# Conditioning units, the scan's steps and the first MLP pairs of a hybrid flow backbone

## The chip, the core and the metric

One core of one Trainium2 chip runs the whole program: a denoising step of a two-layer backbone on 512 latent and 128 context tokens. The metric is the device time of one execution in microseconds (us), the median of several. The engines are TensorE (PE; its weight loads are PEld), VectorE (DVE), ScalarE (ACT), GpSimd (POOL), and SyncE (SP), whose queue issues nearly all DMA transfers in program order.

## What is computed

Each layer computes six conditioning vectors per channel from `c` (and `c_ctx` for the context), a modulated norm, one wide input projection, three token mixers, an output projection, and an MLP with squared ReLU. The kernel gives the same outputs for the tokens, the keys and values and the final scan states:

```
mod = silu(c) @ w_mod[l] + b_mod[l]            # sh1, sc1, g1, sh2, sc2, g2 = split(mod, 6)
h = rmsnorm(x, ln1) * (1 + sc1) + sh1
a_qkv, a_z, a_beta, a_alpha, b_q, b_k, b_v, c_q, c_k, c_v, gates = split(h @ w_in)
ya = gated delta rule, both directions (8 heads of 64, chunks of 64 tokens)
yb, yc = global and windowed attention
x = x + g1 * ((sig(ga)*(ya@w_br_a) + sig(gb)*(yb@w_br_b) + sig(gc)*(yc@w_br_c)) @ w_o)
h2 = rmsnorm(x, ln2) * (1 + sc2) + sh2
x = x + g2 * (square(relu(h2 @ w_ff1)) @ w_ff2)

def step(s, xs):                               # the scan over chunks, s_0 from the context's scan
    u = up_c - w_c @ s
    o = q_c @ s + a_c @ u
    s_new = gl * s + k_c^T @ u                 # = (gl - k_c^T w_c) s + k_c^T up_c
    return s_new, o
```

The conditioning is 12 units per layer of 512 channels each: sh1 and sc1 are units 0 to 3, g1 units 4 and 5, sh2 and sc2 units 6 to 9, g2 units 10 and 11.

## The kernel before

Activations lie feature-major: channels on the 128 partitions, 640 tokens along a row, worked on in two halves of 320. Large products run on pairs of fp32r numbers, a high and a low part, as three products (hi x hi, hi x lo, lo x hi), summed in one PSUM bank. A weight block of fp32 comes by DMA (`fraw`, `graw`, `wraw`), ACT casts it to the high part (L167) and POOL or DVE subtracts that for the low part (L168). Products of the projections appear in the trace as L189 (`gemm_fm`), those of the fills as L422; a product of plain fp32 leaves two PE instructions for each matmul.

**Order.** The program is written in generators that are woven together, and a scheduler then orders each engine's instructions by their priorities and by its own timeline; work with a low priority (`OFF`) goes where the rest leaves room. The low-priority work of a layer is 36 *fills* (`unit`, L415): the parts of the input projection that are needed late. Each takes two weight blocks from a ring of three buffers (`FR`), and SP's nops pace them (L201). DMA issues stand on SP in the order in which the program sets them.

**Conditioning units.** `mod_unit` (L247) sums one unit: eight loads of `w_mod` of 256 KB into the same `fraw` ring, for each four fp32 matmuls of 32 weight columns (L255), then a copy on ACT, a transpose on PE and small adds on DVE (`mod_finish`). In layer 0 units 0 to 3 run at the very start with larger loads. The other eight are low-priority work: unit 4 ahead of all fills (`MP = 1`), and units 5 to 11 one after every fourth fill (`MS = 4`). Layer 1's units run on DVE during layer 0's MLP (`mod_sum`).

**Delta rule.** Four pairs of heads per layer. For each there are the features (convolution and norms), a preparation, a triangular solve, five *posts* (one per 128 tokens, two chunks each), the scan, and the output. The posts of one pair run beside the features and the preparation of the next. `gdn_post` (L608) ends with one bank per chunk that holds the transition matrix of both directions and the additive term; DVE adds the decay to the first (`wm`, L689) and ACT copies the second (`bb`, L690), each as one instruction for both directions, since direction 0 lies on partitions 0 to 63 and direction 1 on 64 to 127. The scan (L698) takes nine steps, seven with a latent chunk of each direction and two for the context. Forward chunk `cf` and backward chunk `cb_` differ, so a step is four products of 64x64 (L712: two heads, two directions) and two adds on DVE of 64 partitions (L716). The states of all chunks stay in `H`; a block of products with `qe` reads them out at the end.

**Output projection and MLP.** `ws` loads the output projection's eight weight blocks through a ring of six buffers and three raw ones; the eight products of the first token half follow, then those of the second, with the next norm between them. The MLP works by pairs of 128-wide hidden blocks. `ff1_plain(p)` takes the two weights of pair p one after the other, each for both halves.

## Time and profile before

| | us |
|---|---|
| median of three runs (lowest, highest) | 2790.38 (2784.02, 2794.83) |
| the profiled execution | 2789.14 |
| its span in the trace | 2787.4 |
| PE busy | 2640.4 (95%) |
| DVE busy | 1986.0 (71%) |
| ACT busy | 1206.7 (43%) |
| POOL busy | 953.4 (34%) |

The stages, as times from the span's start: the start up to the first product of the delta rule; delta rule of layer 0 from 51.7 to 585.7, attention to 890.7, output projection from 922.5 to 982, MLP from 988; in layer 1 the delta rule from 1438.4 to 1978, attention to 2253.8, then projections and MLP up to the end. The fills run within delta rule and attention.

In a row of the timeline, the first number is the start, the second the length of a stretch of like instructions (xN of them), then engine, line, operation, output and inputs by the program's names; in brackets the engine's idle time before it and what ended that. A table of stretches gives for each engine the busy time and the instructions, and PEclk, the granted clock of TensorE as a share of full speed.

### The profile page before, as it was taken

The page shows a single profiled execution, that of the slowest core. Times are in us where ns is not written, and L with a number is a line of the kernel's source. Part 1 is how long each engine was busy: PE and PEld are TensorE (multiplying, and loading weights), DVE is VectorE, ACT ScalarE, POOL GpSimd, SP SyncE. Part 2 cuts the span into 40 slices and gives each one's busy share as a digit, 9 for nine tenths or more (in the row PEclk, how much of TensorE's full clock was granted, in tenths as well). Part 3 has the DMA queues.
Part 4 walks back from the last instruction along what each step waited for, and adds up shares of the span by engine and source line. Part 5 has one row for each costly group of instructions (what it writes and reads, how often), then busy time and mean ns, then how long its engine had stood idle before and what let it go on. Part 6 is the DMA issues. An engine that isn't in the chain of part 4 may idle for free. (4 is left out here: it accounts for less than half of the span.)

```text
span 2787.4 us, 55620 instructions
## 1 busy us (share of the span) xinstructions
PE 2640.4 (95%) x21108; PEld 2450.0 (88%) x21108; DVE 1986.0 (71%) x4253; ACT 1206.7 (43%) x2846; POOL 953.4 (34%) x1259
## 2 busy tenths in 40 slices
PE   5989999999999999999999899899999999999999
PEld 4887888888978999999989888888998789999999
DVE  4587897655557678999966888976556776676564
ACT  3434434445544343444344345344455454343342
POOL 1434434454444211122124445344644630111110
PEclk9999999999999999999999999999999999999999
DMA  7222212333234323554522211112323242222231
GB/s 249 86 89 63 90 47 67 116 118 93 79 103 153 127 79 108 150 159 148 152 85 77 80 48 58 51 48 95 102 72 110 69 154 71 66 85 75 69 99 61
DMA packets 117145, 268.62 MB, mean 96 GB/s; under 512 B 13712, under 2 KB 22544, under 8 KB 116880
## 3 DMA queue, kind: packets, MB, share of 16 engines
q1 hardware_dynamic: 116880, 265.08, 29.8%
q8 instruction: 167, 2.74, 0.4%
q14 instruction: 98, 0.80, 0.1%
HBM read 232.52 MB, written 32.51 MB: 95 GB/s over the span
## 5 line engine op out<-in xcount | busy, mean ns | idle before, releaser
L422 PE MATMUL fm<-hh,fhi 128*128 128x320 f32 x2304 | 446.2, 326 | 17.2 <-SPq L201 8.1
L422 PEld LDWEIGHTS fm<-hh,fhi 128*128 128x128 f32 x2304 | 363.9, 196 | 32.1 <-issue 8.6
L168 POOL TENSOR_TENSOR rl<-fr,rh 128x320 fp32r<-128x320 f32 x128 | 141.5, 1111 | 677.1 <-ACT rh L167 677.0
L168 POOL TENSOR_TENSOR flo<-fraw,fhi 128x512 fp32r<-128x512 f32 x176 | 237.4, 1350 | 306.8 <-ACT fhi L167 189.4
L167 ACT CAST ghi<-graw 128x1024 fp32r<-128x1024 f32 (+1 forms) x148 | 144.9, 980 | 226.1 <-PE gm L1249 128.3
L422 PE MATMUL fm<-hh,flo 128*128 128x320 f32 x1152 | 235.3, 326 | 4.0 <-SPq L201 2.9
L1098 DVE SCALAR_TENSOR_TENSOR x<-gm,mod,x 128x320 f32<-128x320 f32 (+2 forms) x384 | 153.7, 431 | 85.2 <-PE gm L1249 84.5
L1249 PE MATMUL gm<-rh,ghi 128*128 128x320 f32 x1024 | 195.5, 310 | 3.1 <-DVE x L1098 2.9
L1249 PE MATMUL gm<-rl,ghi 128*128 128x320 f32 x1024 | 196.6, 310 | 0.0
L168 DVE TENSOR_TENSOR glo<-graw,ghi 128x1024 fp32r<-128x1024 f32 (+1 forms) x148 | 170.5, 1153 | 35.4 <-ACT ghi L167 18.7
L422 PEld LDWEIGHTS fm<-hh,flo 128*128 128x128 f32 x1152 | 183.8, 195 | 11.0 <-SPq L201 4.8
L1249 PE MATMUL gm<-rh,glo 128*128 128x320 f32 x1024 | 192.0, 309 | 0.0
L167 ACT CAST fhi<-fraw 128x512 fp32r<-128x512 f32 x192 | 119.0, 620 | 162.1 <-PE fm L422 84.9
L189 PE MATMUL mb<-hh,whi 128*128 128x320 f32 x1024 | 167.8, 313 | 3.2 <-ACT whi L167 3.2
L1249 PEld LDWEIGHTS gm<-rh,ghi 128*128 128x128 f32 x1024 | 160.9, 188 | 5.4 <-DVE x L1098 2.4
L1249 PEld LDWEIGHTS gm<-rl,ghi 128*128 128x128 f32 x1024 | 161.7, 188 | 1.0 <-issue 1.0
L1249 PEld LDWEIGHTS gm<-rh,glo 128*128 128x128 f32 x1024 | 160.8, 188 | 0.0
L189 PEld LDWEIGHTS mb<-hh,whi 128*128 128x128 f32 x1024 | 152.5, 188 | 7.2 <-ACT whi L167 4.0
L270 DVE SCALAR_TENSOR_TENSOR macc<-fraw,csil,macc 128x512 f32<-128x512 f32 x168 | 134.9, 820 | 0.2 <-DMA fraw<-w_mod 0.2
L1187 PE MATMUL gm<-hh,ghi 128*128 128x320 f32 x768 | 130.2, 310 | 0.0
L598 DVE TENSOR_TENSOR sv<-sv,stmp 128x31 f32<-128x31 f32 (+15 forms) x248 | 123.4, 498 | 6.5
L961 DVE TENSOR_REDUCE mx<-s 128x1 f32<-128x640 f32 (+3 forms) x160 | 100.1, 632 | 36.6 <-PE s L951 22.6
(326 smaller groups left out, 6210.8 us busy)
## 6 DMA issues: line engine op xcount, KB each, us to landing
graw<-w_ff SPq DMA_DIRECT2D x128, 512.0 KB, 3.5
fraw<-w_mod SPq DMA_DIRECT2D x160, 256.0 KB, 2.8
fraw<-w_fm SPq DMA_DIRECT2D x144, 256.0 KB, 2.8
f_spill<-fgt SPq DMA_DIRECT2D x72, 320.0 KB, 2.2
wraw<-w_fm SPq DMA_DIRECT2D x32, 512.0 KB, 3.5
gts<-f_spill SPq DMA_DIRECT2D x48, 320.0 KB, 3.1
fraw<-w_br SPq DMA_DIRECT2D x48, 256.0 KB, 2.7
graw<-w_o SPq DMA_DIRECT2D x20, 512.0 KB, 4.8
```

The costliest lines, as they stand in the source:

```text
L167: ACT.copy(hi, src)
L168: (lo_eng or DVE).tensor_tensor(out=lo, in0=src, in1=hi.bitcast(F32), op=SUB)
L189: mm = PE.matmul(ps, lhsT=w_[k], rhs=x_[:, k, s], start=(i == 0 and k == 0), stop=(i == 2 and k == n - 1))
L270: stt(out=a, in0=raw, scalar=c, in1=a, op0=MUL, op1=ADD)
L422: mm = PE.matmul(ps[half], lhsT=w[:, k], rhs=x_[:, 4 * q + k, s], start=(q == 0 and k == 0 and w is hi and x_ is hh), stop=(q == 1 and k = ...
L598: tt(out=XX[:, s + 1:32, 0:m], in0=XX[:, s + 1:32, 0:m], in1=tv, op=SUB)
L961: DVE.tensor_reduce(out=mx, in_=pv, axis=AX.XY if n > 512 else AX.X, op=ALU.max)
L1098: stt(out=x[:, j, a:b], in0=ps[:, a - t0:b - t0], scalar=gate[:, j, c:c + 1], in1=x[:, j, a:b], op0=MUL, op1=ADD)
L1187: PE.matmul(ps, lhsT=w_[:, 4 * q + k], rhs=x_[o][:, k], start=(first and i == 0 and k == 0), stop=(i == 2 and k == 3), skip_group_check=True)
L1249: PE.matmul(ps, lhsT=w_[k], rhs=r[k // 2][o][:, k % 2, half_of(half)], start=(i == 0 and k == 0), stop=(i == 2 and k == 3))
```

## The change

Three edits. *Units*: unit 4 no longer runs ahead of the fills (`MP = 0`), units 4 to 7 stand after every eighth fill (`MS = 8`), and units 8 to 11 after the products j = 0, 2, 4 and 6 of the first half of layer 0's output projection. *MLP*: `ff1_plain` takes pairs 0 and 1 together: all four weights for the first token half, then for the second. *Scan*: the transition matrices of step n go into one zeroed tile `wmd`, direction 0 and 1 as the diagonal blocks of a 128x128 matrix in the order of the steps, so that a step is two full-size products, one per head; the states of a step lie in `Hs`, and one add on 128 partitions makes the next. Two copies on ACT (`put`) spread each state into `H` by chunk for the read-out. Posts write each direction into its own place (`STEP_F`, `STEP_B`), so that a chunk takes two adds and two copies where it took one and one; the context's add and copy likewise. The ten buffers of `wm` and `bb` become one `wmd` and one `bbs`.

```diff
@@ -85,7 +85,7 @@
 MB, FM, FB, FR, OFF = 3, 2, 2, 3, 30000
 PACE, PG = 4, 2
 HK = (2, 4, 5)
-MS, MP = 4, 1
+MS, MP = 8, 0
 WRING = 6
 
 
@@ -346,7 +346,7 @@
             for u in range(4):
                 mod_unit(0, u, npool, 2, 6)
             istk.close()
-        mods = [(mod_unit, l, u) for u in range(4, 12)] if l == 0 else []
+        mods = [(mod_unit, l, u) for u in range(4, 8)] if l == 0 else []
         with tc.high_priority(offset=-OFF):
             for f, *a in mods[:MP]:
                 f(*a)
@@ -366,7 +366,7 @@
...
-        GB = dict(zz=2, dd=2, wraw=2, tm=NLB, at=NLB, gss=2, grs=2, sv=3, Y=2, kgb=2, qeg=2, r2=2, gi=2, gsq=2, kq=2, rm=2, rlb=2, ee=2, wm=5, bb=5, qe=5, op=2)
+        GB = dict(zz=2, dd=2, wraw=2, tm=NLB, at=NLB, gss=2, grs=2, sv=3, Y=2, kgb=2, qeg=2, r2=2, gi=2, gsq=2, kq=2, rm=2, rlb=2, ee=2, qe=5, op=2)
...
@@ -657,8 +657,6 @@
                 return Y[:, u, 64:128]
 
             yield
-            wm = gtile([P, 2, 2, 64], "wm")
-            bb = gtile([P, 2, 2, 64], "bb")
             gi = gtile([P, 2, 2, 64], "gi")
             tt(out=gi, in0=bc(egs[:, :, t, h2], 3, 64), in1=bc(bc(i64, 1, 2), 1, 2), op=MUL)
             pqo = bank([P, 3, P], "ma")
@@ -686,41 +684,47 @@
                     PE.matmul(po[64 * h:64 * h + 64], lhsT=yv(u), rhs=AB[:, u], start=(dd == 0), stop=(dd == 1))
             yield
             for c in range(2):
-                tt(out=wm[:, c], in0=pwb[c][:, 0], in1=gi[:, c], op=ADD)
-                ACT.copy(bb[:, c], pwb[c][:, 1])
+                for dd, st in ((0, STEP_F), (1, STEP_B)):
+                    n, o = st[2 * t + c], slice(64 * dd, 64 * dd + 64)
+                    if n is not None:
+                        tt(out=wmd[o, n, :, o], in0=pwb[c][o, 0], in1=gi[o, c], op=ADD)
+                        ACT.copy(bbs[o, n], pwb[c][o, 1])
             yield
             qe = gtile([P, 2, P], "qe")
             ACT.copy(qe, pq)
             ACT.copy(opt[:, t], po)
             busy[pr["ix"]] = dbusy[i] = False
-            res[t] = dict(wm=wm, bb=bb, qe=qe)
+            res[t] = dict(qe=qe)
 
         def gdn_scan(hp, post, opt, oh):
-            H = gtile([P, 10, 2, 64], "H")
+
+            H, Hs = (gtile([P, 10, 2, 64], n) for n in ("H", "Hs"))
             Hf = gtile([P, 2, 64], "Hf")
             h2 = slice(2 * hp, 2 * hp + 2)
-            nc.sync.dma_start(out=H[0:64, 0], in_=d["state"][l, 0:64, h2])
-            nc.sync.dma_start(out=H[64:128, 7], in_=d["state"][l, 64:128, h2])
+            nc.sync.dma_start(out=Hs[:, 0], in_=d["state"][l, :, h2])
+            POOL.memset(Hs[:, 8], 0.0)
             POOL.memset(H[0:64, 8], 0.0)
             POOL.memset(H[64:128, 9], 0.0)
 
-            def step(cf, cb_, of, ob):
+            def put(n, cf, cb_):
+                ACT.copy(H[0:64, cf], Hs[0:64, n])
+                ACT.copy(H[64:128, cb_], Hs[64:128, n])
+
+            def step(n, i, o):
                 ps = bank([P, 2, 64], "ma")
                 for h in range(2):
-                    for dd, c in ((0, cf), (1, cb_)):
-                        s = slice(64 * dd, 64 * dd + 64)
-                        PE.matmul(ps[s, h], lhsT=post[c // 2]["wm"][s, c % 2, h], rhs=H[s, c, h],
-                                  start=True, stop=True)
-                for dd, c, o in ((0, cf, of), (1, cb_, ob)):
-                    s = slice(64 * dd, 64 * dd + 64)
-                    tt(out=o[s], in0=ps[s], in1=post[c // 2]["bb"][s, c % 2], op=ADD)
-
+                    PE.matmul(ps[:, h], lhsT=wmd[:, n, h], rhs=Hs[:, i, h], start=True, stop=True)
+                tt(out=o, in0=ps, in1=bbs[:, n], op=ADD)
+
+            put(0, 0, 7)
             for n in range(7):
-                step(n, 7 - n, H[:, n + 1], H[:, 6 - n])
+                step(n, n, Hs[:, n + 1])
+                put(n + 1, n + 1, 6 - n)
                 if n == 0:
-                    step(8, 9, H[:, 9], H[:, 8])
+                    step(7, 8, Hs[:, 9])
+                    put(9, 9, 8)
                 if n == 1:
-                    step(9, 8, Hf, Hf)
+                    step(8, 9, Hf)
                 yield
             nc.sync.dma_start(out=d["o_state"][l, :, h2], in_=Hf)
             ps, ps2 = bank([P, 4, P], "ma"), bank([P, P], "ma")
@@ -776,7 +780,11 @@
         dbd = [gtile([P, 2, P], f"dbd{i}") for i in range(2 * NBD)]
         abd = [gtile([P, 4, P], f"abd{i}") for i in range(NBD)]
         kzd = [gtile([P, 2, P], f"kzd{i}") for i in range(PD)]
-        for z in lbd + dbd + abd + kzd:
+        wmd = gtile([P, 9, 2, P], "wmd")
+        bbs = gtile([P, 9, 2, 64], "bbs")
+        STEP_F = (0, 1, 2, 3, 4, 5, 6, None, 7, 8)
+        STEP_B = (None, 6, 5, 4, 3, 2, 1, 0, 8, 7)
+        for z in lbd + dbd + abd + kzd + [wmd]:
             POOL.memset(z, 0.0)
         def new_stg():
             stg = gtile([P, 32, 32], "sv")
@@ -1109,6 +1117,8 @@
         nrm = norm(l, 1, 0, x, h2h, h2l, sc)
         for j in range(KC):
             resid(j, 0, gemm_fm(ws[j], mh, ml, 0), L["g1h"])
+            if l == 0 and j in (0, 2, 4, 6):
+                mod_unit(0, {0: 8, 2: 9, 4: 10, 6: 11}[j])
         again = KC - WRING
         order = [*range(again, KC), *range(again)]
         for i, j in enumerate(order):
@@ -1139,13 +1149,13 @@
                     stt(out=t2, in0=src, scalar=0.0, in1=t, op0=ALU.max, op1=MUL)
                 split(r[0][:, c, half_of(half)], r[1][:, c, half_of(half)], t2, POOL)
 
-            def ff1_plain(p):
-                r = rtiles()
-                for c in range(2):
-                    w = wcols(big_w(d["w_ff1"][l, 2 * p + c], DVE), KC)
-                    for half in range(2):
-                        act_square(r, c, half, gemm_fm(w, h2h, h2l, half), False)
-                return r
+            def ff1_plain(*ps):
+                rs = [rtiles() for _ in ps]
+                ws = [wcols(big_w(d["w_ff1"][l, 2 * p + c], DVE), KC) for p in ps for c in range(2)]
+                for half in range(2):
+                    for i, w in enumerate(ws):
+                        act_square(rs[i // 2], i % 2, half, gemm_fm(w, h2h, h2l, half), False)
+                return rs
 
 
             tw = [tuple(fp.tile([P, 4, HALF], F32R, name=f"tw{i}{n}", tag=f"tw{i}{n}") for n in "hl") for i in range(3)]
@@ -1267,11 +1277,11 @@
                             resid(j, half, gemm_r(ws[j], r, half), g2)
 
             nxt = (None, None)
-            prev = ff1_plain(0), ff1_plain(1)
+            prev = ff1_plain(0, 1)
             T1, T2, T3 = ff1_operands()
-            ra = ff1_plain(2)
+            ra, = ff1_plain(2)
             ff2(0, prev, False)
-            prev = ra, ff1_plain(3)
+            prev = ra, *ff1_plain(3)
             T4 = ff1_last_operand()
             for gi_ in range(2, 8):
                 for _ in range(min(2, len(mods))):
```

In the orders below a line with a number of times is that many matmuls. On PE, in the first half of layer 0's output projection (`gm` is the bank of the products, `mh` and `ml` the operand's parts, `fm<-fraw` a conditioning block), before:

```order
L189 MATMUL gm<-mh,ghi 128x320 x43
L189 MATMUL gm<-ml,ghi 128x320 x7
L189 MATMUL gm<-mh,ghi 128x320
L189 MATMUL gm<-ml,ghi 128x320 x7
L189 MATMUL gm<-mh,ghi 128x320
L189 MATMUL gm<-ml,ghi 128x320 x2
L189 MATMUL gm<-mh,glo 128x320 x8
```

and of the change, on the same engine and at the same place:

```order
L189 MATMUL gm<-mh,ghi 128x320 x5
L255 MATMUL fm<-fraw,csil 32x128 x4
L189 MATMUL gm<-mh,ghi 128x320 x5
L255 MATMUL fm<-fraw,csil 32x128
L189 MATMUL gm<-mh,ghi 128x320
L255 MATMUL fm<-fraw,csil 32x128 x3
L189 MATMUL gm<-mh,ghi 128x320
L255 MATMUL fm<-fraw,csil 32x128 x4
L189 MATMUL gm<-mh,ghi 128x320 x18
L255 MATMUL fm<-fraw,csil 32x128 x4
```

The conditioning blocks, four matmuls each, have moved in between products that stood together. On SP at the program's start, after the first loads of units 0 to 3, before:

```order
L252 DMA fraw<-w_mod 128x512 x3
L252 DMA fraw<-w_mod 128x1024 x10
L702 DMA H<-state 64x128
L703 DMA H<-state 64x128
L252 DMA fraw<-w_mod 128x512 x5
L175 DMA fraw<-w_fm 128x512 x6
L175 DMA wraw<-w_fm 128x1024 x2
```

and of the change (the 128x1024 loads are those of units 0 to 3, `w_fm` into `fraw` are fills, into `wraw` the delta rule's own weights):

```order
L175 DMA fraw<-w_fm 128x512 x3
L252 DMA fraw<-w_mod 128x1024 x4
L175 DMA fraw<-w_fm 128x512
L252 DMA fraw<-w_mod 128x1024
L175 DMA fraw<-w_fm 128x512
L252 DMA fraw<-w_mod 128x1024 x5
L704 DMA Hs<-state 128x128
L175 DMA fraw<-w_fm 128x512
L175 DMA wraw<-w_fm 128x1024 x2
```

Unit 4's eight loads of 128x512 are gone from here, and the fills' loads stand between those of units 0 to 3. On DVE, in a post of layer 0's first pair (with what each instruction waits for; the engine's name with a number is its semaphore), before:

```order
L650 COPY_PREDICATED Y<-qswap,ma 128x512 [waits PE_49]
L542 TENSOR_TENSOR tm<-tm,grs 128x256 [waits DVE_49,Pool_49]
L689 TENSOR_TENSOR wm<-ma,gi 128x128 [waits PE_49] x2
L663 TENSOR_TENSOR gi<-egs,cst 128x256 [waits DVE_49]
L629 TENSOR_TENSOR tm<-tm,neg 128x128 [waits Pool_49]
L630 TENSOR_TENSOR tm<-tm,neg 128x128 [waits DVE_49]
```

and of the change:

```order
L650 COPY_PREDICATED Y<-qswap,ma 128x512 [waits PE_49]
L542 TENSOR_TENSOR tm<-tm,grs 128x256 [waits DVE_49,Pool_49]
L690 TENSOR_TENSOR wmd<-ma,gi 64x2x64 [waits PE_49] x2
L690 TENSOR_TENSOR wmd<-ma,gi 64x2x64 [waits Activation_49] x2
L661 TENSOR_TENSOR gi<-egs,cst 128x256 [waits DVE_49]
L629 TENSOR_TENSOR tm<-tm,neg 128x128 [waits Pool_49]
L630 TENSOR_TENSOR tm<-tm,neg 128x128 [waits DVE_49]
```

Where two adds waited for PE alone, there are four, and the second two wait for ACT.

## Rows read from the trace of the kernel before

**Rows 1.** Table of stretches: us, length, busy us of each engine (instructions), PEclk, DMA.
```profile
51.70:585.70 534.00, 491.77 (x4583) 437.54 (x4584) 390.62 (x903) 224.90 (x597) 230.74 (x373) 0.97 0.26 82
585.70:890.70 305.00, 295.30 (x2377) 259.95 (x2375) 181.27 (x432) 155.42 (x412) 147.75 (x155) 0.98 0.32 98
1438.40:1978.00 539.60, 505.95 (x4463) 458.15 (x4462) 402.51 (x921) 234.55 (x618) 242.92 (x394) 0.97 0.21 68
1978.00:2253.80 275.80, 261.06 (x2064) 230.27 (x2062) 180.47 (x432) 146.79 (x394) 138.14 (x147) 0.98 0.27 81
922.50:982.00 59.50, 58.68 (x398) 57.78 (x396) 37.94 (x73) 23.72 (x38) 6.22 (x7) 1.00 0.26 82
```

**Rows 2.** Same table (PE, PEld, DVE, ACT, POOL), one head pair of layer 1.
```profile
1598.00:1645.00 47.00, 46.80 (x546) 40.60 (x546) 32.09 (x95) 29.69 (x90) 27.58 (x53) 1.00 0.14 48
1645.00:1705.00 60.00, 54.69 (x412) 51.26 (x411) 58.12 (x111) 17.57 (x36) 20.46 (x28) 0.94 0.21 69
```

**Rows 3.** Timeline of the start, PE and ACT.
```profile
32.07 0.64 PE L255 MATMUL fm<-fraw,csil 128*32 128x128 f32 x16 [0.55 <-DMA fraw<-w_mod]
33.35 0.64 PE L255 MATMUL fm<-fraw,csil 128*32 128x128 f32 x16 [0.64 <-DMA fraw<-w_mod]
...
50.69 0.62 ACT L167 CAST fhi<-fraw 128x512 fp32r<-128x512 f32 x1 [2.79 <-DMA fraw<-w_fm]
...
53.86 0.62 ACT L167 CAST fhi<-fraw 128x512 fp32r<-128x512 f32 x1 [2.39 <-DMA fraw<-w_fm]
...
68.28 1.00 PE L189 MATMUL mb<-hh,whi 128*128 128x320 f32 x5 [0.85 <-ACT whi L167]
```

**Rows 4.** What L255 waited for, 55 to 700 (us, times), then PE's timeline.
```profile
  DMA fraw<-w_mod: 18.0, 24
...
654.50 0.64 PE L255 MATMUL fm<-fraw,csil 128*32 128x128 f32 x14
655.07 1.31 PE L1008 MATMUL pt<-ph,VT 128*64 128x128 f32 x20
...
657.07 0.43 PE L255 MATMUL fm<-fraw,csil 128*32 128x128 f32 x8
657.43 0.44 PE L951 MATMUL s<-KT,QT 128*128 128x128 f32 x2
```

**Rows 5.** PE's timeline, steps of the scan and a full-size fp32 product.
```profile
257.37 0.68 PE L712 MATMUL ma<-H,wm 64*64 64x64 f32 x16
257.98 1.15 PE L189 MATMUL mb<-hh,wlo 128*128 128x320 f32 x6
...
264.32 0.45 PE L712 MATMUL ma<-H,wm 64*64 64x64 f32 x8
264.70 0.41 PE L189 MATMUL mb<-hh,whi 128*128 128x320 f32 x1
...
1620.47 0.61 PE L648 MATMUL ma<-r,dbd 128*128 128x128 f32 x4
1620.83 0.84 PE L422 MATMUL fm<-hh,fhi 128*128 128x320 f32 x4
```

**Rows 6.** Groups by form: count, busy us, mean ns of one, idle before.
```profile
L689 DVE TENSOR_TENSOR wm<-ma,gi 128x128 f32<-128x128 f32 x80 | 22.0, 287 | 14.4 <-PE ma L677 14.2
L690 ACT COPY bb<-ma 128x128 f32<-128x128 f32 x80 | 20.4, 269 | 21.5 <-DVE wm L689 20.8
```

**Rows 7.** Timeline of a post, ACT and DVE.
```profile
1623.89 0.46 ACT L690 COPY bb<-ma 128x128 f32<-128x128 f32 x2 [1.05 <-DVE wm L689]
...
1625.91 0.58 DVE L689 TENSOR_TENSOR wm<-ma,gi 128x128 f32<-128x128 f32 x2 [0.15 <-PE ma L677]
...
1627.13 0.44 ACT L690 COPY bb<-ma 128x128 f32<-128x128 f32 x2
```

**Rows 8.** PE's timeline ahead of layer 0's MLP.
```profile
984.85 0.78 PE L298 MATMUL gm<-ones,nacc 128*64 128x1 f32 x6 [3.32 <-DVE nacc L293]
...
988.42 1.95 PE L189 MATMUL gm<-hh,ghi 128*128 128x320 f32 x6
```

## The prediction

> **What bounds the kernel now.** I read the table of stretches first, since the whole kernel's 95% of TensorE (PE) hides that its stages have different limits. The stretch of the gated delta rule (head pairs and fill units woven together) and the attention stretch stand there for layer 0 and then layer 1 [rows 1]. In layer 0 they take 534.0 + 305.0 us, in layer 1 539.6 + 275.8. Layer 0 computes seven conditioning units among its fills and layer 1 none; the 23.6 us of difference is in the attention stretch, which holds 313 more PE instructions. So the first stretch doesn't feel the units, and what PE can't do there is left over for attention: about 23.6/7 = 3.4 us a unit. In the output projection PE is busy for 58.68 of 59.50 us [rows 1]: nothing hides there.
>
> The second view is one head pair of layer 1 in two stretches. That with posts and the next pair's preparation (1598 to 1645) keeps PE busy all the time and VectorE (DVE) for two thirds of it; that with the triangular solve, the scan and the next convolution (1645 to 1705) keeps DVE busy for 58.12 of 60 us, and ScalarE (ACT) for a third [rows 2]. So a DVE instruction taken from the scan stretch is worth its time, and one put into the post stretch finds room. Third I read the start, fourth single instructions.
>
> **The sum's base** is the profiled execution, 2789.1 us (span 2787.4 and 1.7 around it); the median of the runs shown is 2790.4, 1.3 more.
>
> **Unit 4 leaves the start.** Before, eight loads of unit 4 go out ahead of the fills' first six weight blocks, since SyncE (SP) issues them in the order of the program. ACT meets the casts of these blocks in the middle of the norm's work and stands for 2.79 and 2.39 us, and the first product of the delta rule comes at 68.28, after a cast of its own weights [rows 3]. The SP order of the change puts the blocks ahead of the last conditioning loads, so 2.79 + 2.39 = 5.2 us of standing go. Against it, five blocks of 256 KB instead of three go ahead of the last loads, which came 1.28 us apart for 512 KB each [rows 3]: 2/2 x 1.28 = 1.3 us later. I take -4 (bounds -6, with PE's own 0.85 in front of that product too, and 0). The 128x2304 memset that the change adds on GpSimd (POOL) stands there too, behind the first two splits; POOL waits for casts at that point, and I cost it at nothing; by DVE's add of 128x128 in 0.287 us [rows 6] eighteen times the elements would take some 5 us, which would count if the third split had to wait for all of it.
>
> **Three units fewer among layer 0's fills** (seven before, four now; unit 4 has gone in there). At 3.4 us each that is -10. From below: PE waited 18.0 us for the blocks of these seven [rows 4], 2.6 a unit, and a group of eight PE instructions (one block, four matmuls, each of which the trace has twice) took 0.36 us [rows 4], 2.9 a unit with eight blocks; 3 x 5.5 = -16. From above: 0, if the attention's own chain sets its length. I take -11.
>
> **Four units in the output projection.** 32 blocks. The PE order sets them singly or in twos and threes between products of 128x320, and no instruction of the stretch waits for anything else, so each adds its time: 0.36 for a single group of eight, 0.57 for fourteen [rows 4], by which an instruction takes 0.035 and a group 0.08 more; and I put 0.05 on the product ahead of a switch. 256 x 0.035 + 26 x 0.08 + 26 x 0.05 = 12.3 us; I take +13 with the four transposes. The blocks share three buffers, and on SP they are queued between the last projection weights and the first MLP weights. Between blocks PE has some 1.9 us on average ((58.68 + 13)/32, less at bunches) and three buffers give three times that before a block is due; SP's own wait there, for a buffer of the projection's weights, holds blocks back only if it lasts longer than that. From above I add the 2.6 us of waiting a unit that they showed among the fills: +23. From below: 256 x 0.035 = +9.
>
> The Trainium skill, TensorEngine Tiling (Array Packing), section Key Properties, says that changing the tiling mode drains TensorE. That speaks against these 26 pairs of switches and for the scan's new form. The rows agree in kind: 0.36 for eight, but 0.57 for fourteen [rows 4], so a fixed part is paid per group; the sum goes by the rows.
>
> **The scan.** Per step, before: four 64x64 products (eight PE instructions) and two DVE adds of 64 partitions; now two products of 128x128 (four instructions), one DVE add of 128 partitions and two ACT copies that set the states out by chunk for the read-out. 9 steps x 8 pairs = 72 steps.
> - PE: 0.38 us for a step alone (264.32 to 264.70), 0.30 in a group of two (257.37 to 257.98), against 0.36 for four full-size instructions (1620.47 to 1620.83) [rows 5], without a switch of shapes on either side (0.05 each, as above). 72 x (0.36 - 0.48) = -8; from above 72 x (0.36 - 0.30) = +4. I take -4, as most steps stand alone.
> - DVE: a step loses one of its two half adds, which I take at the 0.287 us of the posts' add [rows 6]. Nine per scan make 2.6 us per pair, in stretches that DVE bounds [rows 2]; three of four scans per layer lie in such a stretch: 6 x 2.6 = -15.5 in all. The last scan runs while attention starts up; there a shorter step brings perhaps 2 us a layer, inside the bounds below.
> - What is paid for it stands in the posts: 18 adds and 18 copies per pair (each direction into its own block of the zeroed tile) where there were 10 and 10, so 64 more adds of 0.287 (+18.4 us) and, with the scan's 144, 208 more ACT copies of about 0.269 (+56 us) [rows 6]. DVE idles 14.9 of 47 us in a post stretch and ACT 42.4 of 60 in a scan stretch [rows 2]; they cover this.
> - **The new wait.** ACT's copy waits for DVE's add of the same bank already [rows 6], and in the order of the change the second pair of DVE adds waits in turn for ACT. The rows give its price: once ACT stood ready and copied at 1623.89, as soon as DVE let it, once it came at 1627.13, 0.64 after DVE's pair of adds had ended at 1626.49 [rows 7]; with the copy 0.05 to 0.9 us per post, 40 posts: 2 to 36 us of DVE standing. Behind it on DVE wait the preparation of the next pair and then the solve. I take 0.5 x 40 = 20, half of it in time that DVE idles: +10.
>
> Chain of the delta rule: -15.5 + 10 = -5.5. PE is busy for 94% of that stretch (505.95 of 539.6) and fills most gaps, so work that a shorter stretch doesn't hold moves into attention; I let nearly all of it stand all the same, -5, since the waits that go are ones in which PE idles too (54.69 of 60 busy) [rows 1, 2]. With PE's -4 the scan gives -9; bounds -24 (the solves' gain whole, PE -8, no wait) and +24 (36 - 15.5 + 4).
>
> **The MLP by halves**: 0 (+-1). PE's idle time ahead of the MLP, 3.32 us, stands before the norm's own products (984.85), and the MLP's begin at 988.42, when the second half's operands are still being made [rows 8]. In the order of before the scheduler already runs the second weights' first half ahead; PE doesn't wait afterwards. The edit leaves the norm where it was.
>
> Sum: -4 - 11 + 13 - 9 + 0 = -11: 2778 on the profiled execution, **2779** on the median.
>
> **Rivals.**
> 1. Slower: DVE and ACT take turns on the banks in the posts, and each post keeps 0.9 us of it. -4 - 11 + 13 + 4 + (36 - 15.5) = +22.5, about 2813; at 0.6 us kept per post it is +6 (with PE -4). For it: the waits above in the order, ACT busy for 29.69 of 47 us in post stretches [rows 2]; against it: PE has fills to run meanwhile. It decides from 0.45 us on (18 us against 21.5 - 4).
> 2. The units gain nothing where they were and wait where they are: 0 instead of -11, +23 instead of +13, no gain at the start: -9 + 23 = +14, and with half of each +4: 2795 to 2804. For it: 18.0 us of waiting for blocks [rows 4]; against it: three buffers and a wide spacing.
> 3. Faster: the solves' gain is kept whole and ACT is prompt: -4 - 11 + 13 - 20 = -22, and with the units at -16: -27; 2763 to 2768. For it: DVE at 58.12 of 60 us [rows 2].
> 4. Full-size products cost more than packed ones. By the rows of two steps together [rows 5] that is +4 for PE in place of -4: 2787.
>
> On the fourth: the Trainium skill, TensorEngine Tiling (Array Packing), section Theoretical Speedup, gives up to 2x for a dimension of at most 64 from tiles that work side by side, so undoing the packing should cost. In steps that stand alone no run here shows that.
>
> **Chances.** Forecast 0.46, rival 1 0.14, rival 2 0.14, rival 3 0.22, rival 4 0.04. The line of 0.5% (14 us, about what a measurement of this kernel can tell from no change) lies at 2776 and 2804; four tenths of the forecast's cases fall below it. Faster 0.18 + 0.22 = 0.40, same 0.28 + 0.14 + 0.04 = 0.46, slower 0.14. The range 2760 to 2802 takes in rivals 2 to 4 and leaves out most of the first.
>
> **What will show it.** Start: the first product of the delta rule near 64 instead of 68.28. Fills: layer 0's attention stretch some 10 us shorter, layer 1's about as long as before. Output projection of layer 0: near 73 us instead of 59.5, with no waits for conditioning blocks; if they are there, rival 2. Scan stretches 2 to 3 us shorter each, post stretches at most 1.5 us longer; if these grow by 4 us and DVE waits for ACT in the posts, rival 1. The MLP's first 45 us unchanged. The forecast is wrong if the posts' waits pass 18 us in sum, or if the scheduler's new order moves stages that the diff doesn't touch.

## The result

The changed kernel took 2767.45 us, median of four runs (2765.79 to 2769.15), against 2787.2 of the kernel before beside it; the ratio is 0.9919 with a 95% interval of 0.9901 to 0.9937. Run again later it gave 0.9923 (0.9907 to 0.9939). The two medians by themselves lie 19.8 us apart (0.9929, inside the interval); where a run below is given in us without a median, it is the ratio's distance from 1 times 2790, and the difference of its medians can be up to 3 us off that. So the change is faster by 20 to 22 us. The forecast of 2779 had the sign and half of the size, and the time lies inside its range; it is the time of the third rival (2763 to 2768), though not for that rival's reason, as the runs show.

The page of the change, its span and its first section (busy time of each engine, share, instructions):

```profile
span 2764.0 us, 55264 instructions
...
PE 2631.6 (95%) x20820; PEld 2454.3 (89%) x20820; DVE 1989.5 (72%) x4245; ACT 1262.2 (46%) x3054; POOL 977.6 (35%) x1269
```

PE is still busy for 95%, with 288 instructions fewer; ACT has 55 us more, as counted ahead (208 copies of 0.27). Next the table of stretches of the change, with the columns of [rows 1]: delta rule and attention of layer 0, then of layer 1, then the output projection of layer 0.

```profile
43.00:579.40 536.40, 498.08 (x4377) 450.76 (x4378) 399.79 (x922) 259.50 (x719) 246.82 (x393) 0.96 0.23 75
579.40:868.20 288.80, 279.45 (x2253) 246.88 (x2252) 184.27 (x429) 151.28 (x401) 144.64 (x152) 0.99 0.30 94
1429.30:1951.30 522.00, 489.23 (x4266) 451.80 (x4265) 396.92 (x917) 260.42 (x718) 249.52 (x397) 0.98 0.21 69
1951.30:2232.70 281.40, 267.32 (x2117) 235.43 (x2115) 184.82 (x432) 149.18 (x398) 145.22 (x150) 0.99 0.26 83
899.70:974.00 74.30, 74.30 (x653) 64.37 (x651) 37.39 (x78) 23.60 (x40) 4.98 (x5) 1.00 0.55 176
```

Against [rows 1], the pair of stretches of layer 0 went from 839.0 to 825.2 us, that of layer 1 from 815.4 to 803.4, and the output projection from 59.5 to 74.3. The last is 14.8 us for four units, with PE busy all the time.

To see whose time went where, the table below cuts the trace of each kernel at the same five places: the first product of the delta rule in each layer, the first and the last product of layer 0's output projection, and the first of layer 1's. The rest ends with PE's last product, 3.6 to 3.8 us before the span does. The table holds one profiled execution of each kernel; the medians differ from it by up to 2 us here, and by up to 6 in the runs further down.

| us | start | layer 0 to projection | projection | to layer 1's delta rule | layer 1 to projection | rest |
|---|---|---|---|---|---|---|
| before | 68.3 | 854.2 | 59.0 | 479.8 | 822.0 | 500.2 |
| the change | 63.0 | 837.3 | 73.9 | 478.0 | 809.6 | 498.6 |
| scan alone | 67.2 | 849.5 | 63.4 | 480.4 | 811.5 | 501.7 |
| units alone | 63.7 | 839.2 | 74.4 | 478.5 | 818.7 | 501.9 |
| MLP alone | 67.5 | 855.5 | 58.7 | 478.3 | 820.1 | 499.6 |
| unit 4 out of the start | 62.6 | 863.9 | 60.9 | 478.9 | 820.4 | 499.7 |

The start, the projection and layer 1 can be read at once: -5.3, +14.9, -12.4. The second column mixes units and scan, and for that the edits were run one by one.

A few us of a single trace carry little weight. The change run again, the same program, took 835.5 us in the second column and 813.2 in the fifth, 1.8 less and 3.6 more than here. TensorE's granted clock is a part of that: it has two levels, and in layer 0's stretch up to the projection it stood at the lower one, half of the higher, for 37.5 us before, 41.0 in the change, 23.9 with the scan alone, 47.8 with the units alone, 34.1 with the MLP alone and 41.0 with unit 4 out of the start (added up from the traces' clock records). Half of such a difference is the most it can be worth, an estimate for a PE that is busy throughout: some 7 us between scan alone and before.

### The profile page after: what moved, and what is told of

It reads as the page before. It is cut to its first block, busy times and chain, and to the rows that moved or that the text cites. A ratio compares the mean times of both kernels' runs of the same rounds, so it can differ in the third digit from the quotient of the medians.

```text
span 2764.0 us, 55264 instructions
## 1 busy us (share of the span) xinstructions
PE 2631.6 (95%) x20820; PEld 2454.3 (89%) x20820; DVE 1989.5 (72%) x4245; ACT 1262.2 (46%) x3054; POOL 977.6 (35%) x1269
## 5 line engine op out<-in xcount | busy, mean ns | idle before, releaser
L422 PE MATMUL fm<-hh,fhi 128*128 128x320 f32 x2304 | 445.3, 325 | 18.9 <-ACT hh L314 8.3
L422 PEld LDWEIGHTS fm<-hh,fhi 128*128 128x128 f32 x2304 | 359.7, 194 | 32.2 <-ACT hh L314 11.3
L422 PE MATMUL fm<-hh,flo 128*128 128x320 f32 x1152 | 235.4, 324 | 9.2 <-SPq L201 9.1
L422 PEld LDWEIGHTS fm<-hh,flo 128*128 128x128 f32 x1152 | 181.6, 193 | 16.6 <-SPq L201 10.4
L597 DVE TENSOR_TENSOR stmp<-sv 128x31 f32<-128x31 f32 (+15 forms) x248 | 131.0, 528 | 6.1
L977 ACT ACTIVATE p<-s,nb 128x640 f32<-128x640 f32 (+3 forms) x160 | 103.0, 648 | 51.2 <-PE pt L1007 24.9
```

The source lines that it names most:

```text
L422: mm = PE.matmul(ps[half], lhsT=w[:, k], rhs=x_[:, 4 * q + k, s], start=(q == 0 and k == 0 and w is hi and x_ is hh), stop=(q == 1 and k = ...
L597: tt(out=tv, in0=bc(W[:, s + 1:32, s], 2, m), in1=bc(XX[:, s, 0:m], 1, n), op=MUL)
L977: ACT.activation(pw, pv, AF.Exp, bias=nb[:, h:h + 1], scale=0.125, accum_out=den[:, h:h + 1])
```

## Each edit alone

**Scan.** The change without the edits of units and MLP, so that against before only this differs in the steps (and the posts and the tiles that go with it):

```diff
-                        PE.matmul(ps[s, h], lhsT=post[c // 2]["wm"][s, c % 2, h], rhs=H[s, c, h],
-                                  start=True, stop=True)
-                for dd, c, o in ((0, cf, of), (1, cb_, ob)):
-                    s = slice(64 * dd, 64 * dd + 64)
-                    tt(out=o[s], in0=ps[s], in1=post[c // 2]["bb"][s, c % 2], op=ADD)
+                    PE.matmul(ps[:, h], lhsT=wmd[:, n, h], rhs=Hs[:, i, h], start=True, stop=True)
+                tt(out=o, in0=ps, in1=bbs[:, n], op=ADD)
```

> Before with the scan's edit alone. Theory A, from the two traces (layer 1, where no unit runs, lost 12 us between the delta rule's start and the end of attention): 2 x 12 = -24 us, a ratio of 0.9914. Theory B, the recorded sum: -9 us, 0.997. Under A the scan carries the whole gain of the change; under B the rest of it comes from units and MLP.

Measured: 0.9972 (0.9962 to 0.9982), that is -7.8 us. The recorded sum of -9 holds, and the theory formed from the two traces falls: the 12 us that layer 1 lost are not all to be had twice. The table shows why. Layer 1 did lose 10.5 us up to its projection, but layer 0 lost only 4.7, and some of both came back as waiting in the projections. PE's timeline at the start of layer 0's and of layer 1's projection, first of the kernel before, then of this one:

```profile
927.32 2.46 PE L189 MATMUL gm<-mh,ghi 128*128 128x320 f32 x15 [0.35 <-DVE gts L1041]
...
2286.54 4.81 PE L189 MATMUL gm<-mh,ghi 128*128 128x320 f32 x31 [1.34 <-DVE gts L1041]
```

```profile
922.20 6.15 PE L189 MATMUL gm<-mh,ghi 128*128 128x320 f32 x31 [3.54 <-DVE gts L1049]
...
2275.83 4.59 PE L189 MATMUL gm<-mh,ghi 128*128 128x320 f32 x19 [1.86 <-DVE gts L1049]
```

PE waits 3.54 and 1.86 us for the gates' merge on DVE, where the kernel before waits 0.35 and 1.34 us, so some 3.2 us came back in layer 0 and 0.5 in layer 1. In the change there is no such wait in layer 0, where conditioning products stand in the same place.

**Units.** Before with `MS, MP = 8, 0`, units 4 to 7 among the fills and 8 to 11 in the projection:

```diff
-MS, MP = 4, 1
+MS, MP = 8, 0
...
+            if l == 0 and j in (0, 2, 4, 6):
+                mod_unit(0, {0: 8, 2: 9, 4: 10, 6: 11}[j])
```

> Before with the units' edit alone (unit 4 out of the start, three fewer among the fills, four in the output projection). Theory A, from the traces: start -5.3, fills -5.5, output projection +14.8, sum +4 us, 1.0015. Theory B, the recorded sum: -4 - 11 + 13 = -2 us, 0.9993. The stretch of the projection (59.5 us before) should be 74 by both.

Measured: 0.9969 (0.9958 to 0.9979), -8.6 us. Neither theory was near. By the table: start -4.6, layer 0 up to the projection -15.0, projection +15.4, and -2.9 in the rest, in a trace whose last product ends 7.1 us earlier. Three units fewer among the fills are worth 5.0 us each by this trace.

**MLP.** Before with the four weights' first half, then the second:

```diff
-            prev = ff1_plain(0), ff1_plain(1)
+            prev = ff1_plain(0, 1)
```

> Before with the MLP's halves alone. Theory A, from the traces (the MLP's first products stand 1.3 and 1.6 us earlier than the norm in front of them): -3 us, 0.999. Theory B, the recorded sum: 0 (+-1).

Measured: 0.9989 (0.9978 to 1.0001), -3.1 us; the interval reaches zero, so the size isn't secured, but the traces show waits that went. PE's timeline of the kernel before, at the first products of the second matrix in layer 0 and in layer 1:

```profile
1037.27 0.85 PE L1249 MATMUL gm<-rh,ghi 128*128 128x320 f32 x4 [0.66 <-DVE x L1098]
...
2399.29 0.85 PE L1249 MATMUL gm<-rh,ghi 128*128 128x320 f32 x4 [0.96 <-DVE x L1098]
```

and the same place in layer 0 with the edit:

```profile
1036.73 0.75 PE L1249 MATMUL gm<-rh,glo 128*128 128x320 f32 x4
1037.32 0.75 PE L1249 MATMUL gm<-rh,ghi 128*128 128x320 f32 x4
```

Before, a product waited for a bank that DVE's add to `x` had not emptied, 0.66 and 0.96 us, with another short gap behind each. With the edit the groups of four follow each other every 0.59 us. With the gaps that is some 1.2 us in layer 0 and 1.5 in layer 1. Theory A named this size for another place: the MLP's first product, which stands 3.57 us behind the norm's in layer 0 before (988.42 and 984.85) and 4.07 with this edit (989.12 and 985.05).

The three ratios multiply to 0.993, and the change gave 0.9919 and 0.9923. What is left over, 2 to 3 us, is inside the intervals.

**Unit 4 out of the start.** Before with `MP = 0` only, so eight units among the fills and none before them:

```diff
-MS, MP = 4, 1
+MS, MP = 4, 0
```

> Before with unit 4 moved from the start into the fills (eight units there, after every fourth fill) and no other edit. Theory A: the start gives -5.3, a unit more in the fills costs 1.8 (5.5 / 3), sum -3.5 us, 0.9987. Theory B, the recorded terms: -4 + 3.5 = about 0.

Measured: 1.0016 (1.0005 to 1.0027), +4.5 us, against both theories. The start gave its 5.7 us, but one more unit among the fills cost 9.7. Against the units' edit the fills hold four units more and take 24.7 us more: 6.2 a unit.

## What a unit among the fills costs

Before, with one load for each of units 4 to 11, whose block then serves all eight groups of products:

```diff
         for k0 in range(0, KC, nk):
-            raw = (pl or fl).tile([P, nk, 512], F32, name="fraw", tag="fraw", bufs=bufs)
-            nc.sync.dma_start(out=raw, in_=d["w_mod"][l, :, u, k0:k0 + nk])
+            if pl is not None or k0 == 0:
+                raw = (pl or fl).tile([P, nk, 512], F32, name="fraw", tag="fraw", bufs=bufs)
+                nc.sync.dma_start(out=raw, in_=d["w_mod"][l, :, u, k0:k0 + nk])
```

> Before, but each conditioning unit after the first four loads one block instead of eight and uses it for all eight groups of products; leaves out the other loads, so that conditioning values of units 4 to 11 of layer 0 are wrong. Unit 4 stands at the start, so the start gains too, up to 5. Theory D: the 18 us for which TensorE waits for blocks among the fills count in the time: -18 - 5 = -23 us, 0.992. Theory P: they are other idle time under another name (a fill's own waits), and a unit costs its products alone: -5, 0.998.

Measured: 0.992 (0.9907 to 0.9932), -22 us: the loads count. Its trace takes 838.7 us from the first product of the delta rule to the projection, against 854.2, so -15.5 there for the loads of seven units.

The 18.0 us in [rows 4] must be read with care. They add up the idle time of two queues of TensorE, that of its products (PE, 7.3 us) and that of its weight loads (PEld, 10.7 us), which wait for the same blocks at the same time. What the products alone waited for, among the fills (us, times), in the kernel before, in this kernel and in the change:

```profile
  DMA fraw<-w_mod: 7.3, 10
...
  ACT fgt L430: 3.8, 1
...
  DMA fraw<-w_mod: 8.0, 9
```

So PE waited 7.3 us for blocks before, 1.0 a unit. None of that is left in this kernel, though 3.8 us of waiting for a fill's copy have come up. Theory D's -23 was met by -22, but it put 18 us on this wait, and that is luck: the stretch lost twice what PE had waited. The table of stretches from the first product of the delta rule to the projection, before and in this kernel:

```profile
68.30:922.50 854.20, 804.05 (x7089) 715.48 (x7090) 590.03 (x1350) 387.59 (x1015) 386.29 (x529) 0.98 0.30 96
65.20:903.90 838.70, 793.87 (x7086) 712.36 (x7087) 591.36 (x1352) 389.47 (x1017) 384.86 (x530) 0.98 0.25 83
```

PE's idle time fell by 5.3 us only (50.2 to 44.8); its busy time fell by 10.2, with the same products and the same clock. By which path the loads cost the other 8 us stays open. One candidate is SP, which stood 43.0 us for buffers that the units' products held before (26.5 at the units' own loads, 16.5 at those of `w_fm`) and 5.6 here; but its waits at the pacing nops for the fills' products grew from 422.5 to 462.0, so whether that counts isn't shown.

The four units that stay among the fills in the change keep PE waiting as long as the seven did, 8.0 us, and the units' edit alone 6.9; in the projection no product of theirs waits in the change. So a unit costs its products and switches, 3.7 us by the projection (14.9 / 4), and among the fills 5.0 or more. What the change gained by moving units is so mostly the price of work that left a stretch where PE was already the limit (3 x 3.7 of the 15.0 us), and not PE's waits for blocks, which stayed. What the 1.3 us between 3.7 and 5.0 are wasn't separated.

## What the scan's edit is made of

**One add instead of two.** The scan's edit alone, with the step's add in two halves again:

```diff
-                tt(out=o, in0=ps, in1=bbs[:, n], op=ADD)
+                for dd in range(2):
+                    s = slice(64 * dd, 64 * dd + 64)
+                    tt(out=o[s], in0=ps[s], in1=bbs[s, n], op=ADD)
```

> The scan's edit alone (0.9972 of before, -7.8 us), but each step's add on VectorE in two halves of 64 partitions, as before the change; the full-size products stay. 72 more adds of 0.287 us, 20.7 us of VectorE. Theory A (the recorded sum: the shorter chain on VectorE is worth -15.5, the posts cost +10, TensorE gains 4): the gain of the chain goes, 2790 + 8 = about 2798 us, 1.0027. Theory B (TensorE is the limit nearly everywhere, and the whole gain is its 0.106 us a step, 72 x 0.106 = -7.6): the time stays at 0.997, 2782.

Measured: 1.0001 (0.9992 to 1.0011). The whole -7.8 us is gone, so the gain hangs on this add, and theory B falls; both layers lose in the trace, 10.2 us in layer 0 and 6.7 in layer 1 up to their projections. Theory A had the place right and the size at 15.5 where 8.1 came. The groups of the add (columns as in [rows 6]), first before, then in the change:

```profile
L716 DVE TENSOR_TENSOR H<-ma,bb 64x128 f32<-64x128 f32 x128 | 36.7, 287 | 20.0 <-PE ma L712 17.4
```

```profile
L717 DVE TENSOR_TENSOR Hs<-ma,bbs 128x128 f32<-128x128 f32 x64 | 18.3, 285 | 18.2 <-PE ma L716 18.1
```

An add on 64 partitions takes 287 ns and one on 128 takes 285, so half the instructions is half the time: 18.4 us of DVE (the adds into `Hf` stand in a group of their own). Of that, 8.1 us come out of the kernel's time.

Not all of it need be the chain on DVE. With halves TensorE's mean clock over eleven executions is 0.9775, against 0.9784 of the kernel before on the same chip; with the single add it is 0.9811 over eight, against 0.9795. Executions of one and the same kernel show what that goes with: the scan's edit took 2782 to 2783 us at 0.979 and 2775 to 2779 at 0.982 or 0.983, or some 1.3 us for 0.001. By that, an estimate, some 3 of the 8.1 us come by way of the clock, which in the traces with and without halves fell after PE had stood idle. That the shorter chain leaves PE fewer such gaps fits, but isn't shown.

**The turns in the posts.** The scan's edit alone, with a post's two adds ahead of its two copies:

```diff
-                    if n is not None:
-                        tt(out=wmd[o, n, :, o], in0=pwb[c][o, 0], in1=gi[o, c], op=ADD)
-                        ACT.copy(bbs[o, n], pwb[c][o, 1])
+                for n, o in put_at:
+                    if n is not None:
+                        tt(out=wmd[o, n, :, o], in0=pwb[c][o, 0], in1=gi[o, c], op=ADD)
+                for n, o in put_at:
+                    if n is not None:
+                        ACT.copy(bbs[o, n], pwb[c][o, 1])
```

> The scan's edit alone, but a post's two adds on VectorE stand ahead of its two copies on ScalarE, so that VectorE waits for ScalarE no more between them (14.4 us of such waits in the trace of the change). Theory A: the waits count in the chain, -10 against the scan's edit alone: 2772 us, 0.9936. Theory B: they lie beside TensorE's work: 2782 +- 2, 0.997.

Measured: 0.9979 (0.9966 to 0.9991), -5.9 us, no better than the -7.8 of the scan's edit. The groups of the posts' add, in the change, in the scan's edit and then in this kernel:

```profile
L690 DVE TENSOR_TENSOR wmd<-ma,gi 64x128 f32<-64x128 f32 x144 | 39.9, 287 | 27.8 <-ACT bbs L691 14.4 <-PE ma L675 11.2
```

```profile
L690 DVE TENSOR_TENSOR wmd<-ma,gi 64x128 f32<-64x128 f32 x144 | 40.0, 286 | 27.6 <-PE ma L675 15.6 <-ACT bbs L691 9.8
```

```profile
L690 DVE TENSOR_TENSOR wmd<-ma,gi 64x128 f32<-64x128 f32 x144 | 40.8, 287 | 18.7 <-PE ma L675 16.9
```

The wait that the forecast feared is there, 14.4 us in 40 posts of the change or 0.36 a post, under the 0.45 from which it would have decided, and 9.8 us in the scan's edit. Taken away, it gives nothing that can be measured. None of these adds waits for a product of the scan, so the one buffer of `wmd` in place of the five of `wm` holds nothing up.

What the wait costs by itself stays open. This kernel's trace has 865.2 us up to layer 0's projection where the scan's edit has 849.5, and 808.3 against 811.5 in layer 1. The rows of layer 0's stretch, the scan's edit first:

```profile
67.20:916.70 849.50, 800.12 (x6945) 715.59 (x6946) 590.69 (x1345) 414.63 (x1117) 394.50 (x533) 0.99 0.30 96
67.10:932.30 865.20, 809.89 (x6946) 726.85 (x6947) 589.10 (x1347) 418.01 (x1119) 391.84 (x533) 0.97 0.30 95
```

The granted clock is 0.97 against 0.99: the traces have 58 us at the lower level here and 24 there, each time after PE had idled. Half of the difference, 17 us (an estimate, as above), could cover the 15.7 us that this trace is longer.

**The products' size.** The scan's edit alone, with four products of 64x64 on the diagonal blocks of the same tile:

```diff
-                    PE.matmul(ps[:, h], lhsT=wmd[:, n, h], rhs=Hs[:, i, h], start=True, stop=True)
+                    for dd in range(2):
+                        s = slice(64 * dd, 64 * dd + 64)
+                        PE.matmul(ps[s, h], lhsT=wmd[s, n, h, s], rhs=Hs[s, i, h], start=True, stop=True)
```

> The scan's edit alone, but a step's two full-size products again as four of 64x64 on the diagonal blocks; the single add, the copies and the posts stay as in the change. Theory A: TensorE loses its -4 only, 2786 us, 0.9986. Theory B: the whole gain goes, 2790, 1.000. Theory C (the packing rule: small products that lie side by side are cheaper): faster than the scan's edit alone, below 2778, 0.996 or less.

Measured: 0.9962 (0.9948 to 0.9975), -10.6 us, against 0.9972 for the full-size products; the intervals overlap. So the packed products cost nothing against the full-size ones, and may gain. PE's timeline, first with full-size products, then with small ones:

```profile
1644.53 0.89 PE L189 MATMUL mb<-hh,whi 128*128 128x320 f32 x5
1645.26 0.55 PE L716 MATMUL ma<-Hs,wmd 128*128 128x64 f32 x4
1645.63 0.99 PE L189 MATMUL mb<-hh,whi 128*128 128x320 f32 x5
```

```profile
1640.89 1.00 PE L189 MATMUL mb<-hh,whi 128*128 128x320 f32 x5
1641.82 0.68 PE L718 MATMUL ma<-Hs,wmd 64*64 64x64 f32 x16
1642.43 1.89 PE L189 MATMUL mb<-hh,whi 128*128 128x320 f32 x11
```

A full-size step holds PE for 0.37 us, from 1645.26 to 1645.63; two small steps together hold it for 0.61, from 1641.82 to 1642.43. With the slower products on either side a step costs 0.45 us of PE in the one form, and in the other 0.58 alone and 0.405 in a pair (medians of the places in these two traces where products of 128x320 stand on both sides). The scheduler set 13 pairs and 46 single steps here, by which the small products should cost some 5 us more. The runs don't show these 5 us. The scan's edit ran on another chip than this kernel, so each ratio is against the kernel before on its own chip; the two forms side by side follow below.

## The change again, and variants of it

Four kernels on one chip: the change, the change with six units in the projection (6 to 9 in its first half, 10 and 11 in its second), the change with small products, and both together.

```diff
-        mods = [(mod_unit, l, u) for u in range(4, 8)] if l == 0 else []
+        mods = [(mod_unit, l, u) for u in range(4, 6)] if l == 0 else []
...
-                mod_unit(0, {0: 8, 2: 9, 4: 10, 6: 11}[j])
+                mod_unit(0, {0: 6, 2: 7, 4: 8, 6: 9}[j])
...
+            if l == 0 and i in (0, 2):
+                mod_unit(0, 10 + i // 2)
```

> The changed kernel again, beside the three variants on one chip: 0.992 of before. The three edits alone gave 0.9972, 0.9969 and 0.9989, product 0.993. Additive: 0.993, 2770 us; if the edits help one another (in the scan's edit alone the output projection took 63.4 us in layer 0, with all edits 14.9 over 59.0 for its four units): 0.992 or less.

> The change with six conditioning units in the output projection instead of four (units 6 to 9 in its first half, 10 and 11 in its second), so two instead of four among the fills. A unit among the fills cost 5.0 us (15.0 / 3 in the units' edit alone), one in the projection 3.7 (14.9 / 4). Theory U: 2 x (3.7 - 5.0) = -2.6 against the change, 0.991. Theory D, that the units left among the fills carry the waits for blocks (18.0 us for four in the trace of the change): 2 x (3.7 - 3.3 - 4.5) = -8, 0.989. Rival: the projection's loads, 12.6 MB more in 75 us, can't be brought in time and it waits: +5 or more, 0.994.

> The change with the scan's products as four of 64x64 on the diagonal blocks. By the spans in the trace (0.106 us a step) +7.6 against the change, 0.9947; by the run of the scan's edit with small products (0.9962 against 0.9972): 0 to -3, 0.991 to 0.992.

> The change with six units in the projection and small products in the scan. By the two theories that the runs so far favour (U or D, and products of either size alike): 2 to 8 us below the change, 0.989 to 0.991.

| | ratio | interval | median us | layer 0 to projection | projection | to layer 1's delta rule |
|---|---|---|---|---|---|---|
| the change | 0.9923 | 0.9907 to 0.9939 | 2765.93 | 835.5 | 74.4 | 478.0 |
| six units | 0.9928 | 0.9913 to 0.9943 | 2766.28 | 824.6 | 76.6 | 481.9 |
| small products | 0.9915 | 0.9900 to 0.9931 | 2763.21 | 830.9 | 75.4 | 479.0 |
| both | 0.9871 | 0.9850 to 0.9891 | 2752.63 | 816.9 | 76.1 | 481.7 |

Moving two more units took 10.9 us from layer 0's fills and added 2.2 in the projection and 3.9 behind it, -4.8 by the trace, which its median doesn't confirm. Blocks are now waited for, behind the projection's last product and ahead of the MLP, though not at the rival's price: 3.4 us on PE in two waits, here the longer (PE's timeline of six units).

```profile
967.76 0.42 PE L255 MATMUL fm<-fraw,csil 128*32 128x128 f32 x8 [2.07 <-DMA fraw<-w_mod]
```

Small products were once more not dearer. Both together beat both kernels: 0.9871, by the medians 36 us under before and 13 under the change, more than the two apart. Its projection, in the table of stretches:

```profile
880.60:956.70 76.10, 76.08 (x698) 65.01 (x696) 39.14 (x80) 24.69 (x42) 5.35 (x6) 1.00 0.61 194
```

PE is busy for 76.08 of 76.10 us, with DMA at 0.61. Why the two help each other beyond their sum wasn't separated: each edit gives the scheduler a new order, and the clock moves too (layer 0's stretch stood at the lower level for 27.3 us in this trace, for 41.0 in the change and 34.1 in each of the two).

## Why the prediction was right, and where it was off

**Start, -4: right.** Measured -5.3 in the change and -4.6 in the units' edit. ACT's timeline before, at the norm's first part:

```profile
37.06 1.02 ACT L314 ACTIVATE hh<-ntmp,mod 128x320 fp32r<-128x320 f32 x2 [1.41 <-DVE ntmp L312]
```

and ACT's, POOL's and PE's of the change:

```profile
39.77 1.02 ACT L314 ACTIVATE hh<-ntmp,mod 128x320 fp32r<-128x320 f32 x2 [1.55 <-DVE ntmp L312]
...
46.46 2.02 POOL L788 MEMSET wmd<- 128x2304 f32 x1
...
61.86 1.05 ACT L167 CAST whi<-wraw 128x1024 fp32r<-128x1024 f32 x1 [1.34 <-DMA wraw<-w_fm]
62.96 3.20 PE L189 MATMUL mb<-hh,whi 128*128 128x320 f32 x20
```

The first product stands at 62.96 instead of 68.28 [rows 3]. The two waits of 2.79 and 2.39 us are gone, as forecast; the norm begins 2.7 us later, where 1.3 was put. The two terms alone make -2.5, and the rest wasn't followed, so the -4 is in part luck. The new memset took 2.02 us, not 5, and held up nothing that shows here.

**Three units fewer, -11: right in kind, too small.** -15.0 in the units' edit. The term that was off is the price of 3.7 us a unit, which leaned on the attention stretches of the two layers [rows 1]: 5.0 were measured, and 6.2 between eight units and four. The bound from below, 5.5, came nearer, but by luck: its 2.6 us of waiting counts PE and PEld together, where PE alone waited 1.0 a unit, and its 2.9 us of products leave out the switches (3.7 with them, by the projection). The marker named for this term came out at -16.2 in layer 0's attention stretch, with layer 1's 5.6 longer.

**Four units in the projection, +13: right.** +14.9 in the change and +15.4 in the edit alone, where PE waits for blocks not at all and for 1.3 us. The second rival, that they wait there, falls; its 18.0 us were the sum over two queues as well. The 2 us that were missing lie at the switches. PE's timeline of the change:

```profile
904.16 2.90 PE L189 MATMUL gm<-mh,ghi 128*128 128x320 f32 x18
906.99 0.42 PE L255 MATMUL fm<-fraw,csil 128*32 128x128 f32 x8
...
909.83 1.33 PE L189 MATMUL gm<-ml,ghi 128*128 128x320 f32 x8
911.00 1.19 PE L189 MATMUL gm<-mh,glo 128*128 128x320 f32 x7
```

A group of eight took 0.36 us, as in [rows 4]. But 18 products between two groups took 2.83 us, where eight that stand together take 1.17, or 0.146 each: 0.2 us more for the product behind one group and the one ahead of the next, where 0.05 was put on the latter alone.

**Scan, -9: right in sum, wrong in its parts.** -7.8 alone. The chain on DVE was put at -15.5 and the turns in the posts at +10. The add's halves are worth 8.1 in the run, the turns nothing that was seen, and PE's -4 didn't show either, since small products did no worse. The step that was off is that nearly all of the shorter chain stands, although the work that a shorter stretch doesn't hold moves into attention. Where the forecast's markers lay can be read in the same head pair as [rows 2], cut from the first post to the first step and from there to the next pair's first post, before and in the change:

```profile
1598.20:1640.60 42.40, 42.40 (x501) 37.52 (x501) 28.53 (x85) 26.64 (x81) 25.35 (x49) 1.00 0.14 49
1640.60:1705.50 64.90, 59.40 (x458) 54.39 (x456) 61.75 (x120) 20.91 (x47) 22.95 (x32) 0.95 0.20 67
```

```profile
1585.80:1632.30 46.50, 45.70 (x522) 40.10 (x522) 32.84 (x98) 30.99 (x96) 27.42 (x52) 1.00 0.13 44
1632.30:1686.60 54.30, 47.21 (x359) 44.94 (x358) 52.70 (x104) 22.16 (x54) 19.56 (x28) 0.98 0.18 61
```

The posts' stretch grew by 4.1 us, as the first rival said, and the scan's stretch shrank by 10.6, four times what was forecast. DVE shows that work has changed sides: 4.3 us more in the first and 9.1 less in the second. But the halves explain only 9 x 0.287 = 2.6 of these 9.1 us; the rest is other work that the new order has set elsewhere, so the 10.6 is not the chain's own gain. The fills show it on PE, the products of L422 (PE, PEld) in the whole pair, before and in the change:

```profile
1598.20:1705.50 107.30, 39.07 (x204) 33.34 (x204) 0.97 0.18 59
1585.80:1686.60 100.80, 31.13 (x165) 24.95 (x164) 0.99 0.16 53
```

The pair gains 6.5 us and holds 39 products of fills less, which are left for later, and attention gives some of it back (275.8 to 281.4 us in layer 1); what stays is PE's limit. The first rival was right about its place, and its price was paid for by the other stretch.

**MLP, 0: wrong in kind.** -3.1 with an interval up to zero, and -1.8 and -1.6 in the change's trace. The step that failed is the sentence that PE doesn't wait afterwards. It was read at the beginning of the MLP, and the waits stood 50 us later, ahead of the second matrix.

**Full-size products.** The fourth rival put +4 on them in place of -4, from two steps together in [rows 5]. The Trainium skill, TensorEngine Tiling (Array Packing), section Theoretical Speedup, gives packed tiles of at most 64 up to twice the speed. The traces bear that out in small part, and only for steps in pairs (0.405 us a step against 0.45 full-size); in the kernel's time undoing the packing shows no cost clear of the intervals (0.9972 with full-size products, 0.9962 without, and 0.9923 and 0.9915 in the whole change). So neither the -4 nor the +4 was seen.

**The rivals' times.** The third rival gave the time that came, but in part by luck: its units at -16 were right (-15.0), while its scan of -20 measured -7.8. Two of the rivals' sums don't come out of their terms: the first at 0.6 us a post makes +2.5 and not +6, half of the second +1.5 and not +4.

By the ratios the units gave -8.6 where -2 was forecast (4 us of it the price among the fills), the MLP -3.1 where 0 was, the scan -7.8 where -9 was, its errors cancelling: -19.5 in place of -11. The 2 to 3 us from there to the change are inside the intervals.

## What to carry to other kernels

A unit of work in a stretch that its engine limits costs its own time there plus its waits, so price it from its instructions and its waits and not from the difference of two stages that differ in other things too. Read the wait on one engine: a view of a line adds up products and weight loads, and made 18.0 us of 7.3 here. Moving the unit to another stretch with the same limit paid only what it had cost beyond its products and switches, 5.0 against 3.7 us. Where two engines hand a small tile back and forth, count instructions first: halves by partition cost as much as the whole.

## What the runs showed that was not expected

Products of 64x64 in pairs took 0.405 us of PE a step against 0.45 for full-size ones and 0.58 for a single packed step, yet the kernel with mostly single packed steps was not slower. Four conditioning units among the fills kept PE waiting for their blocks for 8.0 us, as long as seven had (7.3), and without the loads the stretch lost twice that. And edits that leave layer 1's program alone changed its length up to the projection by 2 to 3 us (818.7, 820.1 and 820.4 against 822.0). The order of its instructions had shifted, but two executions of the change, with one order, lie 3.6 us apart there (809.6 and 813.2), so a few us of any single trace are no evidence.
